# A third PSUM tile for the expert projections of the gate stage, last-norm weights multiplied before the statistics, an early ACT table load

## The chip, the core and the metric

The kernel runs on one core of a Trainium2 chip. The core has a matrix engine (PE, TensorE), three element-wise engines (DVE or VectorE, ACT or ScalarE, POOL or GpSimd) and an engine that issues transfers (SP or SyncE); ACT and POOL issue transfers too. Each engine runs its own instructions in order and waits on semaphores for the others. The metric is the time of one execution on the device, in microseconds (us).

## The reference

One decoder layer on 512 tokens of width 1024 in float32. Cut to what the change touches:

```python
x = x + mix @ w_out                      # mix: short convolution and gated recurrence of norm(x) @ w_in
h2 = rmsnorm(x, norm_ffn)
# peer_ffn(h2): product-key choice of experts, one neuron each
q = (h2 @ wq).reshape(t, 8, 2, 128)
scores = einsum('thpd,hpnd->thpn', q, keys)
s_top, i_top = top_k(scores, 16)         # two halves of 128 keys each
cand = s_top[:, :, 0, :, None] + s_top[:, :, 1, None, :]
c_score, c_idx = top_k(cand, 16)
expert = i1 * 128 + i2                   # one of 16384
gates = softmax(c_score)
a = gelu(einsum('td,thkd->thk', h2, u_tab[expert]))
y = einsum('thk,thkd->td', gates * a, v_tab[expert])
x = x + y
return rmsnorm(x, norm_f)                # x * rsqrt(mean(x*x) + eps) * norm_f
```

## The kernel before

**Numbers.** Matrix products of float32 data are made of three matmuls (`mm3`, L114 to L117): every operand is split into a high part (`hi`) and a rest (`lo`), and hi·hi, hi·lo and lo·hi are added up in PSUM. `split` (L97) does this for a weight tile of 128x1024: ACT copies it into `whi` (L99) and DVE subtracts to give `wlo` (L101).

**Stages.** The first part (up to about 263 us) makes the mixer. A second (to about 369 us) makes the queries and scores, with the top 16 on DVE. Experts are then handled in two ways. For token block 0 the chosen rows of `u_tab` and `v_tab` are gathered one by one: POOL issues an indirect transfer (L675) into a ring of 8 raw slots, and DVE multiplies and adds (L681 for u, L689 for v). For the 384 tokens of blocks 1 to 3 the whole tables are used: `uchunk(c)` (L440) makes Gelu(u·h2) of 128 experts for 384 tokens, 24 matmuls of 128x384 and one ACT Gelu (`gl`, L447), and for early chunks a transfer `Ad<-gl` (L449) spills it. The dense gates for these tokens are built by `gate_m`, 24 times: DVE makes one-hot tables A, B1 and, multiplied by the gate's rest and high part, B2 (L646) and B1 (L647), then PE multiplies them into four PSUM tiles of 8 matmuls each (L656, L657), and ACT evicts each tile into `stg` (L659); every second call sends `stg` to DRAM (L662). Scores and gates live in the pool `psS`, opened before the query loop and closed before the main stage; the chunks U1 to U86 are woven between them. I call 264 to 797 us the gate stage. From about 797 us the main stage multiplies gates and Gelu outputs with `v_tab`, up to 1488.8 us, and `finish` adds the residual and makes the last norm.

**PSUM in the gate stage.** Eight banks: two tiles "a" in `psA`, which the chunks use in turn, and six tiles "m" in `psS` for scores and gates. So the matmuls of chunk n wait for the Gelu of chunk n-2. ACT is in order: that Gelu comes after whatever was put ahead of it, gate evictions and `whi` copies of later chunks among them.

**The order.** The program is written out as loops in the file; a scheduler of the framework then sets the order in which each engine gets its instructions.

**Start and end.** At the start ACT waits for the first piece of the input, loads its function table, scales the input to `hThi` (L155) and copies the first weight. In `finish` (before: L793 to L807) each token block needs, for each half of 512 columns: residual add on DVE (L799), sum of squares on ACT (L800); then the reciprocal root in small steps (`rstd_of`), and a scalar_tensor_tensor (STT) on DVE for each half (L806) that multiplies by the root and by the norm's weights `nfb`.

Of the kernel before, what the change touches and what calls it, by code (L numbers as in the profile page):

```python
# [10 lines left out]
F32 = mybir.dt.float32  # L11
# [4 lines left out]
AF = mybir.ActivationFunctionType  # L16
OP = mybir.AluOpType
AX = mybir.AxisListType
PSUM = bass.MemoryType.PSUM
DRAM = bass.MemoryType.DRAM  # L20

P = 128
T = 512
D = 1024
# [8 lines left out]
TD = T - P  # L33
# [21 lines left out]
def body(ctx, tc, a):  # L55
    nc = tc.nc
    V, S, G, PE = nc.vector, nc.scalar, nc.gpsimd, nc.tensor
# [7 lines left out]
    sm = sb("sm", 2)  # L65
    dr = sb("dr", space=DRAM)
    psA = sb("psA", 2, space=PSUM)
# [9 lines left out]
    ones = const("ones", [P, 2])  # L77
# [16 lines left out]
        V.scalar_tensor_tensor(o, q, 1.5, r, op0=OP.add, op1=OP.mult)  # L94
        return o

    def split(src):  # L97
        hi = ws.tile([P, D], F32R, tag="hi", name="whi")
        S.activation(hi, src, AF.Copy)  # L99
        lo = ws.tile([P, D], F32R, tag="lo", name="wlo")  # L100
        V.tensor_sub(lo, src, hi.bitcast(F32))  # L101
        return hi, lo

    def wunit(src):
# [4 lines left out]
    ring = [None]  # L109
# [6 lines left out]
        PE.matmul(out, l[0], r[1], start=False, stop=False)  # L116
        PE.matmul(out, l[1], r[0], start=False, stop=last)  # L117

    sm.tile([P, 104], F32, name="pad", bufs=1)
    hT = (hp.tile([P, ND, T], F32R, tag="hi", name="hThi"), hp.tile([P, ND, T], F32R, tag="lo", name="hTlo"))  # L120
    x1d = dr.tile([NB, P, D], F32, name="x1d")
    h2d = dr.tile([P, D], F32, name="h2d")
# [23 lines left out]
    wraw = []  # L146
    for i in range(4):
        nc.sync.dma_start(out=xT[i], in_=a["xt"][:, 2 * i:2 * i + 2, :])
        wraw.append(ring[0]())
        nc.sync.dma_start(out=wraw[i], in_=a["w_in"][16 + i])  # L150
    G.memset(ones, 1.0)

    def make_h(dc):
        t = xT[dc // 2][:, dc % 2, :]
# [16 lines left out]
    wf = []  # L171
    for i in range(4):
        make_h(2 * i)
        make_h(2 * i + 1)
        wf.append(split(wraw[i]))
    for t, nm in ((scanm, "scanm"), (maskc, "maskc"), (gmask, "gmask")):
        S.dma_start(out=t, in_=a[nm])
    pf = [ps() for h in range(HG)]
# [46 lines left out]
    for h in range(HG):  # L225
        o = proj(12 + h)
# [17 lines left out]
    for h in range(HG):  # L244
        o = proj(24 + h)
# [143 lines left out]
    c = conv_c(0)  # L389
    for tb in range(NB):  # L390
        hgrn_pre(tb)
    for tb in range(NB):
# [8 lines left out]
        if tb < NB - 1:  # L401
            c = conv_c(tb + 1)
# [3 lines left out]
    nfb = fp.tile([P, D], F32, tag="v", name="nfb")  # L406
# [32 lines left out]

    def uchunk(c):  # L440
        w = wunit(a["u_l"][c])
        o = psA.tile([P, T], F32, tag="a", name="pa")[:, :TD]
        for dc in range(ND):
            sl = slice(dc * P, (dc + 1) * P)
            mm3(o, (w[0][:, sl], w[1][:, sl]), (h2T[0][:, dc, P:], h2T[1][:, dc, P:]), dc == 0, dc == ND - 1)
        gl = mp.tile([P, TD], F32, tag="gl", name="gl", bufs=LAG + 1)
        S.activation(gl, o, AF.Gelu)  # L447
        if c < SPILL:
            S.dma_start(out=Ad[c], in_=gl)  # L449
        return gl  # L450

    h2T = (hp.tile([P, ND, T], F32R, tag="hi", name="h2Thi"), hp.tile([P, ND, T], F32R, tag="lo", name="h2Tlo"))
    h2s = [fp.tile([P, D], F32, tag=t, name="h2s") for t in ("gs", "Q", "G", "E1")]
# [43 lines left out]
    S.dma_start(out=h2n, in_=h2d)  # L497
    G.memset(y0, 0.0)
    sel = ExitStack()
    psS = sel.enter_context(tc.tile_pool(name="psS", bufs=6, space=PSUM))  # L500
    raw_ring(sel.enter_context(tc.tile_pool(name="rs", bufs=1)), 8)
    sp = sel.enter_context(tc.tile_pool(name="sp", bufs=1))
    s2 = sel.enter_context(tc.tile_pool(name="s2", bufs=2))
# [218 lines left out]
    gls = {}  # L722
    for k in range(LAG):
        gls[SPILL + k] = uchunk(SPILL + k)
    sel.close()


# [65 lines left out]
    def finish(tb, ys):  # L793
        xx = xs[tb]
        ms = sm.tile([P, 2], F32, tag="fms", name="fms")
        jk = ring[0]()
        for hf in range(2):
            cs = slice(hf * T, (hf + 1) * T)
            V.tensor_add(xx[:, cs], xx[:, cs], ys[hf])  # L799
            S.activation(jk[:, cs], xx[:, cs], AF.Square, accum_out=ms[:, hf:hf + 1])  # L800
        m = sm.tile([P, 1], F32, tag="m1", name="m1")
        V.tensor_add(m, ms[:, 0:1], ms[:, 1:2])
        r = rstd_of(m, 1.0 / D, 1, "f")
        for hf in range(2):
            cs = slice(hf * T, (hf + 1) * T)
            V.scalar_tensor_tensor(xx[:, cs], xx[:, cs], r[:, 0:1], nfb[:, cs], op0=OP.mult, op1=OP.mult)  # L806
            nc.sync.dma_start(out=a["out"][tb * P:(tb + 1) * P, cs], in_=xx[:, cs])  # L807

    xs = []
    for tb in range(NB):  # L810
# [58 lines left out]
```

## Time and profile before

| | us |
|---|---|
| median of three runs | 1501.52 (1498.21 to 1503.9) |
| the profiled execution, its own time | 1500.03 |
| span of its trace (first to last instruction) | 1498.1 |
| PE busy | 1462.3 (98%) |
| DVE busy | 1201.3 (80%) |
| ACT busy | 637.0 (43%) |
| POOL busy | 365.8 (24%) |
| PE idle on a chunk's Gelu, whole gate stage | 12.4 in 8 waits |

The profiled execution lies 1.5 us under the median of the three runs. Busy shares are an average over stages; "PE busy" counts a matmul that runs at half clock as busy for its whole length, so the granted clock has to be read beside it. A row of a timeline gives the start, the length, the engine, the line, the operation with output and inputs, and in brackets the idle time before it and what ended it.

### The profile page before, as it was taken

To read this page: it belongs to the slowest core of one execution; us is meant where nothing else is said; L and a number is where in the kernel's file an instruction comes from. 1 tells how busy PE (TensorE), PEld (TensorE's weight loads), DVE (VectorE), ACT (ScalarE), POOL (GpSimd) and SP (SyncE) were. 2 spreads that over 40 slices of the span, in tenths; PEclk is the share of its full clock that TensorE was granted. 3 is DMA by queue.
4 is the path that set the end of the run, shared out by engine and by line. 5 is a ranking of instruction groups with operands and counts; after the bars stand their busy time and mean duration, and the time that the engine had idled before them with its cause. 6 is when DMAs were issued, how large, how long until landed. Compare 5 with 4: busy or idle time off the path is not lost.

```text
span 1498.1 us, 21741 instructions
## 1 busy us (share of the span) xinstructions
PE 1462.3 (98%) x7929; PEld 1297.3 (87%) x7929; DVE 1201.3 (80%) x2312; ACT 637.0 (43%) x900; POOL 365.8 (24%) x284
## 2 busy tenths in 40 slices
PE   7999999999998999999999999999999999999997
PEld 6887777888998998889999999999998888888886
DVE  5847876799989988788829878778787788888887
ACT  5833324333443365666744333333333333333333
POOL 0000000000034142320014445444343224333340
PEclk9999999999999999999999999999999999999999
DMA  6231233622469789689779999998989999999993
GB/s 230 85 106 43 70 127 112 246 86 90 161 209 386 244 279 315 231 293 321 261 287 419 324 337 323 338 341 313 345 298 338 368 369 368 355 356 352 352 342 118
DMA packets 137770, 394.64 MB, mean 263 GB/s; under 512 B 13120, under 2 KB 59584, under 8 KB 135488
## 3 DMA queue, kind: packets, MB, share of 16 engines
q1 hardware_dynamic: 47520, 170.94, 31.5%
q0 software_dynamic: 39168, 159.40, 29.4%
q10 hardware_dynamic: 50976, 62.93, 11.9%
q8 instruction: 62, 1.02, 0.3%
q14 instruction: 44, 0.36, 0.1%
HBM read 346.82 MB, written 46.40 MB: 262 GB/s over the span
## 4 chain that ended last, share of the span: by engine, by line
PE 76%; DVE 6%; ACT 5%; issue 5%; DMA 5%; POOL 2%; ACTq 1%; POOLq 0%; DVEq 0%
PE y L116 10%; PE y L115 10%; PE y L117 10%; PE pa L115 8%; PE pa L116 7%; PE pa L117 7%; PE pm L115 7%; PE pm L116 6%; PE pm L117 6%; ACT stg L659 4%; DMA wraw<-in_v_dram,e_i 2%; POOL wraw L675 2%; DVE wlo L101 2%; DMA wraw<-in_u_dram,e_i 1%; PE pm L538 1%
## 5 line engine op out<-in xcount | busy, mean ns | idle before, releaser
L99 ACT ACTIVATE whi<-wraw 128x1024 fp32r<-128x1024 f32 x308 | 325.8, 1058 | 518.4 <-PE pa L116 205.4
L101 DVE TENSOR_TENSOR wlo<-wraw,whi 128x1024 fp32r<-128x1024 f32 x308 | 376.2, 1222 | 144.8 <-ACT whi L99 141.1
L115 PE MATMUL pa<-h2Thi,whi 128*128 128x384 f32 x1024 | 348.0, 340 | 12.7 <-ACT gl L447 12.4
L117 PE MATMUL pa<-h2Thi,wlo 128*128 128x384 f32 x1024 | 346.6, 338 | 0.0
L116 PE MATMUL pa<-h2Tlo,whi 128*128 128x384 f32 x1024 | 346.2, 338 | 0.0
L675 POOL DMA_INDIRECT wraw<-in_u_dram,e_i x128 | 183.3, 1432 | 490.2 <-DVE ci L523 178.6
L116 PE MATMUL y<-wlo,wh 128*128 128x512 f32 x768 | 299.5, 390 | 0.0
L115 PE MATMUL y<-whi,wh 128*128 128x512 f32 x768 | 298.9, 389 | 0.2 <-ACT wh L747 0.2
L117 PE MATMUL y<-whi,wl 128*128 128x512 f32 x768 | 296.8, 390 | 0.0
L675 POOL DMA_INDIRECT wraw<-in_v_dram,e_i x128 | 169.4, 1323 | 263.2 <-DVE wlo L101 122.0
L115 PEld LDWEIGHTS pa<-h2Thi,whi 128*128 128x128 f32 x1024 | 194.3, 190 | 17.8 <-ACT gl L447 15.9
L116 PEld LDWEIGHTS pa<-h2Tlo,whi 128*128 128x128 f32 x1024 | 194.4, 190 | 1.6
L117 PEld LDWEIGHTS pa<-h2Thi,wlo 128*128 128x128 f32 x1024 | 194.1, 190 | 0.0
L681 DVE SCALAR_TENSOR_TENSOR wraw<-wraw,h2n 128x1024 f32<-128x1024 f32 x128 | 155.9, 1219 | 34.7 <-DMA wraw<-in_u_dram,e_i 34.6
L689 DVE SCALAR_TENSOR_TENSOR y<-wraw,w,y 128x1024 f32<-128x1024 f32 x128 | 163.9, 1280 | 17.1 <-DMA wraw<-in_v_dram,e_i 16.9
L117 PEld LDWEIGHTS y<-whi,wl 128*128 128x128 f32 x768 | 144.1, 188 | 30.2
L115 PEld LDWEIGHTS y<-whi,wh 128*128 128x128 f32 x768 | 144.2, 188 | 29.7 <-ACT wh L747 0.6
L116 PEld LDWEIGHTS y<-wlo,wh 128*128 128x128 f32 x768 | 144.1, 188 | 29.0
L747 ACT ACTIVATE wh<-w 128x384 fp32r<-128x384 f32 x128 | 65.8, 522 | 208.2 <-PE y L116 97.6
L659 ACT ACTIVATE stg<-pm 128x512 f32<-128x512 f32 x96 | 92.3, 1156 | 17.7 <-PE pm L657 17.7
L749 DVE TENSOR_TENSOR wl<-w,wh 128x384 fp32r<-128x384 f32 x128 | 70.2, 554 | 22.8 <-ACT wh L747 22.3
L115 PE MATMUL pm<-hThi,whi 128*128 128x512 f32 x192 | 77.7, 406 | 8.4 <-ACT whi L99 8.4
(240 smaller groups left out, 1694.7 us busy)
## 6 DMA issues: line engine op xcount, KB each, us to landing
wraw<-in_u_l_dram SPq DMA_DIRECT2D x128, 512.0 KB, 5.6
wraw<-in_v_l_dram SPq DMA_DIRECT2D x128, 512.0 KB, 6.4
Gd<-stg ACTq DMA_DIRECT2D x12, 2048.0 KB, 7.6
Gt<-Gd POOLq DMA_DIRECT2D x16, 1536.0 KB, 9.7
Ad<-gl ACTq DMA_DIRECT2D x84, 192.0 KB, 5.0
glr<-Ad ACTq DMA_DIRECT2D x84, 192.0 KB, 5.2
wraw<-in_w_in_dram SPq DMA_DIRECT2D x24, 512.0 KB, 3.7
wraw<-in_wq_dram SPq DMA_DIRECT2D x16, 512.0 KB, 7.4
```

The costliest lines, as they stand in the source:

```text
L99: S.activation(hi, src, AF.Copy)
L101: V.tensor_sub(lo, src, hi.bitcast(F32))
L115: PE.matmul(out, l[0], r[0], start=first, stop=False)
L116: PE.matmul(out, l[0], r[1], start=False, stop=False)
L117: PE.matmul(out, l[1], r[0], start=False, stop=last)
L538: PE.matmul(o[:, tb * NK:(tb + 1) * NK], q[:, tb * P:(tb + 1) * P], keys[:, i, :], start=True, stop=True)
L659: S.activation(st[:, t0:t0 + 4, :], o3, AF.Copy, scale=1.0 / GSC)
L675: G.indirect_dma_start(out=t, out_offset=None, in_=a[tab], in_offset=bass.IndirectOffsetOnAxis(ap=e_i32[:, j:j + 1], axis=0))
L681: V.scalar_tensor_tensor(r, r, 1.0, h2n, op0=OP.mult, op1=OP.mult, accum_out=act0[:, j:j + 1])
L689: V.scalar_tensor_tensor(y0, r, w0[:, j:j + 1], y0, op0=OP.mult, op1=OP.add)
L747: S.activation(wh, w, AF.Copy)
L749: V.tensor_sub(wl, w, wh.bitcast(F32))
```

## The change

1. `psS` gets five banks for scores and gates. The sixth becomes a tile "u", and while the gate stage lasts every third chunk (c % 3 == 2) uses it; the other chunks go on using the two tiles of `psA`. Chunk n then waits for the Gelu of the chunk three before it.
2. In `finish` both halves of x are multiplied by `nfb` into a second buffer `xm` (from the same raw ring) as soon as the residual is added. After the root, half 0 is scaled on DVE by a tensor_scalar and half 1 on ACT by a Copy with a scale.
3. A tiny ACT Copy of `ones` stands ahead of everything that waits for data, so that ACT's table is loaded there. The first weight is split in four pieces of 256 columns. A pad tile shrinks from 104 to 96 columns.

```diff
-    def split(src):
+    def split(src, n=1):
         hi = ws.tile([P, D], F32R, tag="hi", name="whi")
-        S.activation(hi, src, AF.Copy)
         lo = ws.tile([P, D], F32R, tag="lo", name="wlo")
-        V.tensor_sub(lo, src, hi.bitcast(F32))
+        for i in range(n):
+            cs = slice(i * D // n, (i + 1) * D // n)
+            S.activation(hi[:, cs], src[:, cs], AF.Copy)
+            V.tensor_sub(lo[:, cs], src[:, cs], hi[:, cs].bitcast(F32))
         return hi, lo
...
-    sm.tile([P, 104], F32, name="pad", bufs=1)
+    sm.tile([P, 96], F32, name="pad", bufs=1)
...
     G.memset(ones, 1.0)
+    S.activation(sm.tile([P, 2], F32, name="warm", bufs=1), ones, AF.Copy)
...
-        wf.append(split(wraw[i]))
+        wf.append(split(wraw[i], 1 if i else 4))
...
     def uchunk(c):
         w = wunit(a["u_l"][c])
-        o = psA.tile([P, T], F32, tag="a", name="pa")[:, :TD]
+        o = upsum(c)[:, :TD]
...
+    in_sel = [False]
+
+    def upsum(c):
+        if in_sel[0] and c % 3 == 2:
+            return psS.tile([P, T], F32, tag="u", name="pa", bufs=1)
+        return psA.tile([P, T], F32, tag="a", name="pa")
...
-    psS = sel.enter_context(tc.tile_pool(name="psS", bufs=6, space=PSUM))
+    psS = sel.enter_context(tc.tile_pool(name="psS", bufs=5, space=PSUM))
+    in_sel[0] = True
...
+    in_sel[0] = False
     sel.close()
...
     def finish(tb, ys):
         xx = xs[tb]
         ms = sm.tile([P, 2], F32, tag="fms", name="fms")
-        jk = ring[0]()
+        jk, xm = ring[0](), ring[0]()
         for hf in range(2):
             cs = slice(hf * T, (hf + 1) * T)
             V.tensor_add(xx[:, cs], xx[:, cs], ys[hf])
             S.activation(jk[:, cs], xx[:, cs], AF.Square, accum_out=ms[:, hf:hf + 1])
+            V.tensor_mul(xm[:, cs], xx[:, cs], nfb[:, cs])
...
-            V.scalar_tensor_tensor(xx[:, cs], xx[:, cs], r[:, 0:1], nfb[:, cs], op0=OP.mult, op1=OP.mult)
-            nc.sync.dma_start(out=a["out"][tb * P:(tb + 1) * P, cs], in_=xx[:, cs])
+            if hf:
+                S.activation(xm[:, cs], xm[:, cs], AF.Copy, scale=r[:, 0:1])
+            else:
+                V.tensor_scalar(xm[:, cs], xm[:, cs], r[:, 0:1], None, op0=OP.mult)
+            nc.sync.dma_start(out=a["out"][tb * P:(tb + 1) * P, cs], in_=xm[:, cs])
```

The lines after the change have other numbers: about 3 more in the first part (L155 becomes L158, L447 becomes L450), 11 more in the gate stage (L646 becomes L657, L659 becomes L670).

Where the order changes, first ACT at the start of the program, before and then after. `warm` is the new tiny copy, `E` the buffer for squares.

```order
L145 DMA prm<-in_prm_dram 128x33
L145 DMA ident<-in_ident_dram 128x128
L177 DMA scanm<-in_scanm_dram 128x512
L155 ACT_TABLE_LOAD
L155 ACTIVATE hThi<-F,prm 128x512 x2
L177 DMA maskc<-in_maskc_dram 128x128
L177 DMA gmask<-in_gmask_dram 128x128
L99 ACTIVATE whi<-wraw 128x1024
```

```order
L147 DMA prm<-in_prm_dram 128x33
L147 DMA ident<-in_ident_dram 128x128
L154 ACT_TABLE_LOAD
L154 ACTIVATE warm<-ones 128x2
L180 DMA scanm<-in_scanm_dram 128x512
L158 ACTIVATE hThi<-F,prm 128x512 x2
L180 DMA maskc<-in_maskc_dram 128x128
L180 DMA gmask<-in_gmask_dram 128x128
L102 ACTIVATE whi<-wraw 128x256 x4
```

The table load now stands ahead of everything that waits for `F`, and one transfer, `scanm`, has gone behind it.

Second, ACT at the first pair of gate calls, before and then after: `stg<-pm` is the eviction of a gate tile, `gl<-pa` a chunk's Gelu.

```order
L99 ACTIVATE whi<-wraw 128x1024
L447 ACTIVATE gl<-pa 128x384
L449 DMA Ad<-gl 128x384
L659 ACTIVATE stg<-pm 128x4x128 x8
L99 ACTIVATE whi<-wraw 128x1024
L662 DMA Gd<-stg 128x16x256
L447 ACTIVATE gl<-pa 128x384
```

```order
L102 ACTIVATE whi<-wraw 128x1024
L450 ACTIVATE gl<-pa 128x384
L452 DMA Ad<-gl 128x384
L670 ACTIVATE stg<-pm 128x4x128 x5
L102 ACTIVATE whi<-wraw 128x1024
L670 ACTIVATE stg<-pm 128x4x128
L450 ACTIVATE gl<-pa 128x384
L670 ACTIVATE stg<-pm 128x4x128 x2
L452 DMA Ad<-gl 128x384
L673 DMA Gd<-stg 128x16x256
```

The eight evictions in a row have become five, with a weight copy and a Gelu among the last three.

Third, DVE at the seventh and eighth gate call, before and then after: `A` and `B` are the one-hot tables, `y` the v rows of block 0, `oh` work on the next block's choice.

```order
L605 TENSOR_TENSOR oh<-oh 128x32x8
L644 TENSOR_TENSOR A<-iota,gt 128x2048
L645 TENSOR_TENSOR B_5087<-iota,gt 128x2048
L689 SCALAR_TENSOR_TENSOR y_2163<-wraw,w_2161,y_2163 128x1024
L644 TENSOR_TENSOR A<-iota,gt 128x2048
L645 TENSOR_TENSOR B_5206<-iota,gt 128x2048
L646 TENSOR_TENSOR B_5088<-B_5087,gt 128x2048
L101 TENSOR_TENSOR wlo<-wraw,whi 128x1024
```

```order
L616 TENSOR_TENSOR oh<-oh 128x32x8
L655 TENSOR_TENSOR A<-iota,gt 128x2048
L656 TENSOR_TENSOR B_5095<-iota,gt 128x2048
L700 SCALAR_TENSOR_TENSOR y_2171<-wraw,w_2169,y_2171 128x1024
L657 TENSOR_TENSOR B_5096<-B_5095,gt 128x2048
L655 TENSOR_TENSOR A<-iota,gt 128x2048
L656 TENSOR_TENSOR B_5214<-iota,gt 128x2048
L658 TENSOR_TENSOR B_5095<-B_5095,gt 128x2048
```

The seventh call's first product (L646 before, L657 after) has moved ahead of the eighth call's two tables.

## Rows read from the trace of the kernel before

**Rows 1.** First page: busy time by engine.

```profile
PE 1462.3 (98%) x7929; PEld 1297.3 (87%) x7929; DVE 1201.3 (80%) x2312; ACT 637.0 (43%) x900; POOL 365.8 (24%) x284
```

**Rows 2.** What PE waited for, 430 to 765 us: total, times, longest.

```profile
PE pa L115 <- ACT gl L447: 12.4, 8, 4.2
PE pm L656 <- DVE B L646: 1.8, 1, 1.8
```

**Rows 3.** The first of these, 702 to 765 us alone.

```profile
PE pa L115 <- ACT gl L447: 2.0, 2, 1.6
```

**Rows 4.** Stretches: busy us by engine (instructions), granted clock, DMA share, GB/s.

```profile
454.50:461.30 6.80, 5.03 (x16) 5.03 (x17) 6.80 (x18) 2.20 (x3) 3.22 (x3) 0.50 0.95 350
461.30:500.00 38.70, 38.70 (x225) 38.67 (x224) 36.29 (x65) 14.31 (x20) 10.96 (x7) 1.00 0.99 374
635.40:642.30 6.90, 6.10 (x21) 5.79 (x22) 6.90 (x7) 2.18 (x4) 1.27 (x1) 0.51 1.06 403
```

**Rows 5.** Timeline of PE at the two longest waits on a Gelu.

```profile
451.76 0.34 PE L117 MATMUL pa<-h2Thi,wlo 128*128 128x384 f32 x1
456.27 0.69 PE L115 MATMUL pa<-h2Thi,whi 128*128 128x384 f32 x1 [4.17 <-ACT gl L447]
...
636.20 0.69 PE L115 MATMUL pa<-h2Thi,whi 128*128 128x384 f32 x1 [3.19 <-ACT gl L447]
```

**Rows 6.** Timeline of ACT and its queue at the same two places.

```profile
453.16 0.31 ACT L565 ACTIVATE g<-g 128x128 f32<-128x128 f32 x1 [6.41 <-DVE g L564]
...
628.53 6.08 ACTq L449 DMA_DIRECT2D Ad<-gl  x1
634.71 1.06 ACT L99 ACTIVATE whi<-wraw 128x1024 fp32r<-128x1024 f32 x1 [5.26 <-issue]
```

**Rows 7.** Timelines of PE and DVE at two gate calls.

```profile
593.51 0.40 PE L656 MATMUL pm<-B,A 128*128 128x128 f16 x4 [1.79 <-DVE B L646]
...
592.24 1.22 DVE L646 TENSOR_TENSOR B<-B,gt 128x2048 f16<-128x2048 f16 x1
...
701.65 0.40 PE L656 MATMUL pm<-B,A 128*128 128x128 f16 x4
...
699.96 2.35 DVE L646 TENSOR_TENSOR B<-B,gt 128x2048 f16<-128x2048 f16 x2
```

**Rows 8.** What DVE waited for, 453 to 702 us (first four).

```profile
DVE wraw L681 <- DMA wraw<-in_u_dram,e_i: 19.7, 7, 4.9
DVE y L689 <- DMA wraw<-in_v_dram,e_i: 5.7, 3, 4.5
DVE A L644 <- ACT gt L629: 4.3, 2, 3.1
DVE wlo L101 <- ACT whi L99: 3.0, 6, 0.9
```

**Rows 9.** Timelines of POOL and DVE at one gather.

```profile
543.53 9.03 POOL L675 DMA_INDIRECT wraw<-in_u_dram,e_i  x1 [10.57 <-DVE y L689]
...
556.12 1.23 DVE L681 SCALAR_TENSOR_TENSOR wraw<-wraw,h2n 128x1024 f32<-128x1024 f32 x1 [4.37 <-DMA wraw<-in_u_dram,e_i]
```

**Rows 10.** Timeline of ACT: the first pair of gate calls.

```profile
529.75 7.75 ACT L659 ACTIVATE stg<-pm 128x512 f32<-128x512 f32 x8 [2.60 <-PE pm L657]
```

**Rows 11.** Timelines of ACT and PE at the start.

```profile
4.73 1.28 ACT L155 ACT_TABLE_LOAD   x1 [4.73 <-DMA F<-in_xt_dram]
6.03 1.33 ACT L155 ACTIVATE hThi<-F,prm 128x512 fp32r<-128x512 f32 x2
7.27 1.04 ACT L99 ACTIVATE whi<-wraw 128x1024 fp32r<-128x1024 f32 x1
...
8.36 0.79 PE L115 MATMUL pm<-hThi,whi 128*128 128x512 f32 x1 [8.36 <-ACT whi L99]
```

**Rows 12.** Timeline of DVE at the end.

```profile
1490.74 1.41 DVE L806 SCALAR_TENSOR_TENSOR wraw<-wraw,vo,nfb 128x512 f32<-128x512 f32 x2
...
1493.52 1.41 DVE L806 SCALAR_TENSOR_TENSOR wraw<-wraw,vo,nfb 128x512 f32<-128x512 f32 x2
```

## The prediction

> **What bounds the kernel now.** I read the first page first: it says which engine fills the span. PE is busy 98% of it and the next engine, DVE, 80% [rows 1]. So a change gains only what it takes from PE's idle time, from stretches in which PE runs at half clock, or from the start and end where PE has nothing to do. The list of PE's waits comes next. Between 430 and 765 us, in the gate stage, PE stood 12.4 us in 8 waits for a chunk's Gelu (`gl`), and 1.8 us once for a gate table of DVE [rows 2]. The windows of the same stage show a second loss: right after the two long waits the granted clock is 0.50 and 0.51, the 1.2 GHz level, where the stretch after the first has 1.00 [rows 4]. Before each of these falls PE had stood idle, 4.17 and 3.19 us by its timeline [rows 5].
>
> The two timelines of ACT say why PE stood. At the first place ACT itself waited 6.41 us for DVE to deliver `g`, the gate's softmax input, and the Gelu that PE needed came after it, so that PE went on at 456.27 [rows 5, 6]. At the second place the issue of one spill transfer took 6.08 us, and ACT's next instruction began at 634.71 [rows 6]. Neither has to do with PE. PE was stopped because a chunk may begin only when the Gelu of the chunk two before it is done. In both cases it would have had other chunks to do.
>
> **Part 1, the third tile: the ceiling.** A chunk is 24 matmuls; in the stretch from 461.3 us at full clock PE did 225 in 38.70 us, 0.172 us each [rows 4], so a chunk is some 4.1 us of PE work. With three tiles a Gelu may be one chunk later before PE stops. The stalls are 4.17 and 3.19 us and smaller ones, so almost all of the 12.4 us would go; of the first I leave 0.3 us, since ACT must also copy the weights of the chunk that PE would run in the gap. What the low clock costs: between 454.5 and 461.3 PE was busy 5.03 us, between 635.4 and 642.3 it was busy 6.10 us [rows 4], and at half clock half of that is lost, 2.5 and 3.05 us. Ceiling: 12.4 - 0.3 + 2.5 + 3.05 = 17.7 us.
>
> **Why I take less.** PE can be earlier only if what else it needs is earlier too. In this stage it also needs the gate tables of DVE, and DVE is in order and has its own waits. At 593.51 PE already waits 1.79 us for a table that DVE ends 592.24 + 1.22 = 593.46; at 701.65 it starts on one whose two products run from 699.96 to 702.31, of which the first ends about 701.1, so PE has about half a microsecond in hand there [rows 7]. The change puts this first product about 2.3 us earlier on DVE, but the gate matmuls about 2.6 us earlier on PE too, so the margin stays. What is gained before 593 or before 702 is then kept only as far as DVE also comes earlier. DVE's waits say how far that can be. Between 453 and 702 us 25.4 us (19.7 + 5.7) are waits for gathered rows, 3.0 us for `whi` and 4.3 us for `gt`, both from ACT [rows 8]. The waits for `whi` end earlier with PE, since a `whi` buffer comes free when PE is done with it: 3.0 us. The waits for `gt` hang on PE (transposes) and ACT: I take 3 of 4.3. The gathers I take as staying as they are: their transfers are issued by POOL as DVE frees the slots, and one of them needed 9.03 us to be issued while DVE worked on [rows 9]. So up to 702 us the gain is 3 + 3 = 6 us. Behind 702 the stalls on Gelus are 2.0 us [rows 3], with no near table in the way; they are added. **Gate stage: -8 us**, bounds -3 (only the waits for `whi`) and -17.7 (ceiling). Between ends so far apart I take the value nearer to the low one, because the row at 593.51 shows the cap already reached before the change.
>
> On the 9.03 us, the Trainium skill (SBUF — State Buffer, the box on "DVE blocks DMA" under "two separate sides") says that descriptors of a transfer issued by GpSimd cannot be written while VectorE runs an operation in a two-port mode, and that the transfer then appears blocked. By that rule the gathers would follow DVE wherever it goes, and its 25.4 us would not shrink. The trace agrees only in part: the issue spans DVE's work and ends where DVE stops and waits 4.37 us, yet a later section of the page doubts that the operations DVE runs there count.
>
> **Part 1, the price: a bank fewer for the gates.** Two gate calls make eight tiles in a row; ACT evicted the eight in 7.75 us, 0.97 us each [rows 10]. With five banks the sixth tile waits for the first eviction. In the new order matmuls of a chunk stand ahead of the sixth tile, about six of them, 6 x 0.172 = 1.0 us, as much as one eviction takes. That is the work that hides it; with that cover I price it at nothing. Without it each pair would lose up to two evictions, 1.9 us. ACT's order moves the same way: five evictions together, then a weight copy and a Gelu among the others. The scores of the stage before share these five banks; I price that at nothing too, since the same evictions and the same cover hold there, and a loss belongs to the slower rival below.
>
> **Part 3, the start.** ACT got its table at 4.73, after waiting for the first input, and that load took 1.28 us [rows 11]. Now it lies in the wait for data, so the first copies are 1.28 us earlier. The first weight copy took 1.04 us as one [rows 11]; in quarters PE can begin after the first, some 0.6 us sooner, an estimate. PE would then begin at about 6.5 in place of 8.36. But PE runs out of weights again: each further weight needs about 3.4 us of ACT (two input copies 1.33, the weight 1.04 [rows 11], and a square of the weight's shape, the same again by estimate), and its transfer besides, which comes no earlier. Bounds 0 and -1.9; I take -0.6. The Trainium skill (ScalarE: Activation LUTs, "What ACT_TABLE_LOAD costs") gives some 2.66 us for a switch, with a drain; by that the upper bound would be -3.3. The trace disagrees: the load is 1.28 us, and the next copy starts 1.30 us after it began [rows 11].
>
> **Part 2, the end.** The last block's two STTs took 1.41 us [rows 12]. A tensor_scalar on DVE and a Copy on ACT, side by side, take about half, so -0.7. Against it stand two extra multiplications per block, at an STT's half of 0.7 us each; those of the last block run while ACT squares and takes the root. The block before loses its pair of STTs too (1.41 us at 1490.74) and gains one tensor_scalar, and DVE runs it in order ahead of the last block's root. I take -0.3; bounds -0.7 and +1.4 (both multiplications not hidden).
>
> **Sum.** -8 - 0.6 - 0.3 = -8.9 us. Against the profiled execution: 1500.0 - 8.9 = 1491.1, span 1498.1 to 1489.2. The median of the runs lies 1.5 us above the profiled one, so the predicted median is 1501.5 - 8.9 = 1492.6, rounded to **1492.5 us**. A measurement can tell about 0.5%, 7.5 us, from no change; the forecast lies just beyond.
>
> **The rivals.**
> - *The full ceiling.* DVE comes earlier as well, because its gathers are issued earlier along with it and the waits for `gt` go. For it: DVE waits there, it isn't full (80%) [rows 1]. Against it: PE's wait at 593.51. Gain 13 to 17.7 plus 0.9: around 1485 us.
> - *VectorE keeps its pace.* What PE gains on Gelus it gives back as longer waits for tables, and a longer wait for a table may drop the clock just as the waits on Gelus did. Then the gate stage gains 0 to 5, of it 2.0 behind 702 for certain. For it: the wait at 593.51, the margin at 701.65 and the 25.4 us of gather waits; the rule of the skill above would make it so. Time 1496 to 1501, with 1498.5 in the middle.
> - *Slower: five gate banks are too few.* The cover of chunk matmuls fails, because those matmuls themselves wait, or ACT's evictions come later behind the weight copy that now stands between them. Price: two evictions of 0.97 us per pair, 12 pairs, 23.3 us; with -8.9 from the rest +14.4, about 1516 us. It decides when a pair loses over 8.9 / 12 = 0.74 us; slower by over 0.5% from (8.9 + 7.5) / 12 = 1.4 us per pair.
> - *The tile doesn't do what it says.* If chunks wait for operands rather than for the Gelu, the third tile stays empty. Against it: where PE stood before a chunk, the wait list names the Gelu, 12.4 us of it, and never `whi` or `wlo` [rows 2]. Its time is that of the second rival's upper end, and its chance lies there.
>
> **How the numbers follow.** My forecast (gate stage gains 5 to 13): 0.50. Full ceiling: 0.12. VectorE keeps its pace: 0.30. Slower by five banks, at any size: 0.08. Faster by over 0.5% needs a gain over 7.5 us: all of the ceiling, 0.12, and three quarters of the forecast's chance, 0.38, which gives 0.50. Within 0.5%: the rest of the forecast, 0.12, and the second rival, 0.30, which gives 0.42. Slower 0.08. The range runs from 1484 (near the ceiling's 1501.5 - 18.6 = 1482.9, the last of it left out) to 1502 (the second rival with nothing gained and something lost at the end); the slower rival and the tip of the ceiling stay outside, about 1 in 10. The forecast's own range, for gate gains of 5 to 13, is 1487.6 to 1495.6.
>
> **What would show it.** In the list of PE's waits the Gelu falls from 12.4 us to 1 or so, and waits for gate tables of DVE grow from 2 to 5 to 10 us; if they don't grow, the ceiling holds. The half-clock stretches near 454 and 635 go, or come back behind a wait for a table. DVE's waits for gathers in the stage stay near 25 us. The sixth tile of a pair doesn't show a wait for an eviction; if it does in most pairs, the slower rival holds. At the start PE begins near 6.5; at the end the last output follows the last matmul by a little less. The prediction is wrong if the gate stage, from the first chunk to the main stage, is shorter by under 5 or over 13 us.

## The result and the profile after

| | before | after |
|---|---|---|
| median | 1503.54 us (1498.21 to 1505.03, 6 runs) | 1493.79 us (1492.01 to 1496.41, 6 runs) |
| profiled execution | 1500.03 us, span 1498.1 | 1494.14 us, span 1491.9 |

The ratio is 0.994, with a 95% interval of 0.9923 to 0.9956: 9.75 us by the medians, where 8.9 were forecast. The two profiled executions stand only 5.9 us apart, because that of before is on the fast side of its runs. The trace answers for these two executions. I cut them at four places that both have: the first matmul of chunk U1, the 145th matmul into a `y` tile (a point in the main stage with the same 2927 matmuls behind it in both), the end of the last matmul, and the end of the span.

| stretch | before, us | after, us | difference |
|---|---|---|---|
| start to U1 | 363.57 | 362.19 | -1.38 |
| gate stage, U1 to the 145th `y` matmul | 499.65 | 492.41 | -7.24 |
| from there to the last matmul's end | 625.58 | 628.63 | +3.05 |
| last matmul's end to the span's end | 9.30 | 8.67 | -0.63 |
| sum | 1498.10 | 1491.90 | -6.20 |

From here on "gate stage" is the second of these stretches; a list of waits names its own window.

Busy time, first page of the kernel after (it answers to [rows 1]): 

```profile
PE 1460.3 (98%) x7929; PEld 1292.9 (87%) x7929; DVE 1200.9 (80%) x2319; ACT 639.6 (43%) x908; POOL 368.7 (25%) x284
```

The shares don't move, so nothing is to be read from them. What PE waited for does move; the same list, 430 to 765 us, for the kernel after (answers to [rows 2]; total, times, longest):

```profile
PE pm L667 <- DVE B L657: 5.5, 3, 2.2
PE pa L117 <- ACT gl L450: 1.7, 1, 1.7
PE pm L668 <- DVE B L658: 1.5, 2, 1.3
PE pa L119 <- DVE wlo L103: 0.5, 1, 0.5
```

Waits on a Gelu are down from 12.4 us to 1.7. Waits on the gate tables are up from some 2 to 5.5 + 1.5 = 7.0 us. No wait on the eviction of a gate tile is in the list. The windows at half clock (they answer to [rows 4]):

```profile
467.00:470.40 3.40, 3.40 (x13) 3.40 (x12) 3.40 (x11) 1.98 (x3) 0.54 (x1) 0.50 1.04 420
586.40:589.80 3.40, 3.08 (x13) 3.09 (x14) 3.40 (x4) 0.82 (x2) 0.00 (x0) 0.50 1.08 408
```

Two stretches of 3.40 us are left of two of 6.8. PE was busy 3.40 + 3.08 us in them and lost half, 3.2 us, where it had lost 5.6. Both still come behind a wait of PE, as its timeline shows, the first on a Gelu, the second on a table. Not every wait is followed by one: behind those of 1.77, 1.27 and 1.48 us between 634 and 655 us the granted clock stayed at 1.00.

```profile
465.28 0.44 PE L117 MATMUL pa<-h2Thi,whi 128*128 128x384 f32 x1 [1.74 <-ACT gl L450]
...
586.72 0.50 PE L667 MATMUL pm<-B,A 128*128 128x128 f16 x3 [2.24 <-DVE B L657]
```

These terms give the stage: Gelus -10.7, tables +4.9, `wlo` +0.5, clock -2.3, together -7.6, against -7.24 measured.

At the first of the two old stalls ACT stands as long as before, but PE no longer does. Timeline of ACT after (answers to [rows 6]):

```profile
451.37 0.31 ACT L576 ACTIVATE g<-g 128x128 f32<-128x128 f32 x1 [6.00 <-DVE g L575]
...
463.80 1.06 ACT L102 ACTIVATE whi<-wraw 128x1024 fp32r<-128x1024 f32 x1 [1.94 <-DMA wraw<-in_u_l_dram]
```

ACT's wait of 6.00 us for `g` was covered. A short one came 14 us later, when PE had run ahead of the weights' transfers and ACT waited for them; the DMA engines were full there (share 1.04 in the window at 467 above).

The late tables stand behind gathered rows. In VectorE's timeline the table of the wait at 586.72 ends 586.66, and since its 4.12 us for a row VectorE has not paused:

```profile
579.49 1.23 DVE L692 SCALAR_TENSOR_TENSOR wraw<-wraw,h2n 128x1024 f32<-128x1024 f32 x1 [4.12 <-DMA wraw<-in_u_dram,e_i]
...
585.44 1.22 DVE L657 TENSOR_TENSOR B<-B,gt 128x2048 f16<-128x2048 f16 x1
```

The other three of over 1 us come the same way, without a pause of VectorE in between: those at 634.78 and 641.60 behind a wait of 4.21 us for a row that ended at 621.21, that at 653.67 behind one of 3.97 us that ended at 646.65.

In the main stage PE has two waits that before did not have (list, 797 to 1485 us). The first, at 1134.81, stands behind a row of block 0 that VectorE waited 4.01 us for, the second, at 1140.18, behind that and a load of gates (`Gt`, 0.80 us). They are 3.0 us, against +3.05 for the stretch:

```profile
PE y L119 <- DVE wl L761: 1.5, 1, 1.5
PE y L117 <- ACT wh L759: 1.5, 1, 1.5
```

Start and end, timelines of ACT, PE and DVE after (answer to [rows 11, 12]):

```profile
1.67 1.28 ACT L154 ACT_TABLE_LOAD   x1 [1.67 <-PEq L877]
4.93 0.72 ACT L158 ACTIVATE hThi<-F,prm 128x512 fp32r<-128x512 f32 x1 [1.77 <-DMA prm<-in_prm_dram]
6.17 1.32 ACT L102 ACTIVATE whi<-wraw 128x256 fp32r<-128x256 f32 x4
...
6.63 0.79 PE L117 MATMUL pm<-hThi,whi 128*128 128x512 f32 x1 [6.63 <-ACT whi L102]
...
1486.78 0.49 DVE L822 TENSOR_SCALAR wraw<-wraw,vo 128x512 f32<-128x512 f32 x1
...
1485.92 1.58 ACT L820 ACTIVATE wraw<-wraw,vo 128x512 f32<-128x512 f32 x2 [0.18 <-issue]
```

The table load lies in the wait for data, and PE begins 1.73 us earlier. The last block's scaling is 0.49 us on DVE beside 0.72 on ACT, in place of 1.41. It ends 4.27 us after the last matmul, in place of 6.13, so 1.86 us sooner; the span's end gains only 0.63. The DMA share says where the rest stays: after, the last six outputs follow each other without a pause and fill the DMA engines, where before there were gaps between them. First the kernel after, then before:

```profile
1486.00:1490.00 4.00, 0.00 (x0) 0.00 (x0) 1.13 (x6) 1.36 (x2) 0.00 (x0) 0.69 1.02 390
...
1492.00:1494.00 2.00, 0.00 (x0) 0.00 (x0) 1.50 (x8) 0.20 (x1) 0.00 (x0) 0.54 0.68 262
1494.00:1495.00 1.00, 0.00 (x0) 0.00 (x0) 0.94 (x2) 0.00 (x0) 0.00 (x0) 0.50 0.00 0
```

### The profile page after: what moved, and what is told of

The parts are those of the page before. It is cut to its first block, busy times and chain, and to the rows that moved or that the text cites. A ratio compares the mean times of both kernels' runs of the same rounds, so it can differ in the third digit from the quotient of the medians.

```text
span 1491.9 us, 21767 instructions
## 1 busy us (share of the span) xinstructions
PE 1460.3 (98%) x7929; PEld 1292.9 (87%) x7929; DVE 1200.9 (80%) x2319; ACT 639.6 (43%) x908; POOL 368.7 (25%) x284
## 4 chain that ended last, share of the span: by engine, by line
PE 46%; issue 7%; DMA 5%; POOL 2%; DVE 2%; ACT 0%; POOLq 0%; ACTq 0%; DVEq 0%
PE y L117 10%; PE y L119 10%; PE y L118 10%; PE pa L119 5%; PE pa L118 5%; PE pa L117 5%; DMA wraw<-in_v_dram,e_i 3%; POOL wraw L686 2%; DMA wraw<-in_u_dram,e_i 1%; PE pm L667 1%; PE pm L668 1%; DMA Gt<-Gd 1%; DVE wlo L103 0%; DMA wraw<-in_v_l_dram 0%; DVE B L656 0%
## 5 line engine op out<-in xcount | busy, mean ns | idle before, releaser
L102 ACT ACTIVATE whi<-wraw 128x1024 fp32r<-128x1024 f32 (+1 forms) x311 | 325.9, 1049 | 506.6 <-PE pa L118 189.6
L103 DVE TENSOR_TENSOR wlo<-wraw,whi 128x1024 fp32r<-128x1024 f32 (+1 forms) x311 | 376.0, 1210 | 142.1 <-ACT whi L102 133.5
L700 DVE SCALAR_TENSOR_TENSOR y<-wraw,w,y 128x1024 f32<-128x1024 f32 x128 | 163.7, 1279 | 14.1 <-DMA wraw<-in_v_dram,e_i 13.7
L670 ACT ACTIVATE stg<-pm 128x512 f32<-128x512 f32 x96 | 94.3, 1159 | 19.2 <-PE pm L668 19.1
```

Of the source, the lines that this page charges most:

```text
L102: S.activation(hi[:, cs], src[:, cs], AF.Copy)
L103: V.tensor_sub(lo[:, cs], src[:, cs], hi[:, cs].bitcast(F32))
L670: S.activation(st[:, t0:t0 + 4, :], o3, AF.Copy, scale=1.0 / GSC)
L700: V.scalar_tensor_tensor(y0, r, w0[:, j:j + 1], y0, op0=OP.mult, op1=OP.add)
```

## The experiments

Twelve kernels, each against runs of the kernel before on the same chip. The last columns are read from each one's trace as in the table above; "half clock" is the time at 0.50 between 264 and 797 us.

| kernel | ratio (95%) | median, us | gate stage, us | half clock, us |
|---|---|---|---|---|
| before | 1 | 1502.4 to 1503.5 | 499.65 | 13.6 |
| after | 0.994 (0.9923 to 0.9956) | 1493.79 | 492.41 | 6.8 |
| p1_tile | 0.9942 (0.9927 to 0.9957) | 1492.54 | 490.88 | 3.4 |
| p23_ends | 0.998 (0.9967 to 0.9993) | 1500.29 | 499.94 | 10.2 |
| five_banks | 0.9949 (0.9937 to 0.9962) | 1495.75 | 495.54 | 10.2 |
| four_banks | 0.9963 (0.9946 to 0.998) | 1497.32 | 497.14 | 13.6 |
| two_u | 0.9926 (0.9898 to 0.9954) | 1491.13 | 489.78 | 3.4 |
| light_b1 | 0.99 (0.9885 to 0.9916) | 1489.17 | 492.31 | 13.6 |
| no_gather | 0.9841 (0.9813 to 0.9868) | 1477.75 | 478.72 | 0 |
| no_gather_b | 0.9895 (0.9878 to 0.9912) | 1487.30 | 485.20 | 0 |
| early36 | 1.0063 (1.0042 to 1.0084) | 1510.63 | 487.42 | 3.4 |
| lag2 | 0.9952 (0.9933 to 0.9972) | 1493.90 | 492.06 | 6.8 |
| lag2_two | 0.9946 (0.9927 to 0.9965) | 1493.04 | 488.51 | 3.4 |
| lag1_two | 0.994 (0.9919 to 0.9962) | 1492.95 | 490.76 | 3.4 |

How far can one trace be trusted? lag2 runs the instructions of the kernel after on PE, ACT, DVE and POOL in the same order, one for one; its gate stage is 492.06 us against 492.41. two_u, lag1_two and lag2_two share another order: 489.78, 490.76 and 488.51. So between single traces of this stage a difference of some 2 us shows nothing.

### The parts alone

The third tile alone (p1_tile) is the kernel after with the old start and `finish`:

```diff
-            V.tensor_mul(xm[:, cs], xx[:, cs], nfb[:, cs])
...
-    S.activation(sm.tile([P, 2], F32, name="warm", bufs=1), ones, AF.Copy)
...
-        wf.append(split(wraw[i], 1 if i else 4))
+        wf.append(split(wraw[i]))
```

> Only the third PSUM tile and the five gate banks; start and end as before. Theory (the gain comes from the gate stage, where PE no longer stands for a Gelu two chunks back, cut short by VectorE's tables): first matmul at 8.36 us as before, PE's waits on a chunk's Gelu at most 3 us in place of 12.4, its waits on gate tables 5 to 10 us, chunk U85 begins 6 to 8 us earlier than before, and the time is 6 to 9 us under before. Rival (the gain is mainly in the start and the end): under 3 us gained.

Measured: 0.9942, ten us under before by the medians, the gate stage 8.8 us shorter. PE's waits (430 to 765 us) are 0.4 us on Gelus, 6.3 on tables and 2.4 on a weight. That is as much as the whole change gives.

Start and end alone (p23_ends) are the kernel after without the tile:

```diff
-    psS = sel.enter_context(tc.tile_pool(name="psS", bufs=5, space=PSUM))
-    in_sel[0] = True
+    psS = sel.enter_context(tc.tile_pool(name="psS", bufs=6, space=PSUM))
```

> Only the early table load, the first weight in four pieces and the new finish; PSUM as before. Theory: first matmul near 6.6 us, the first chunk after the scores begins about 1.4 us earlier than before, the end after the last matmul is 8.7 us in place of 9.3, PE's waits on a chunk's Gelu stay at 10 to 14 us, and the time is about 2 us under before (1 to 3). Rival (the start is lost again before the gate stage because the weights come no earlier): at most 1 us.

Measured: 0.998, some 3 us by the ratio, with an interval from 1 to 5. First matmul at 6.63, end 8.83 us after the last matmul. But U1 began at 363.58, as before: of the 1.73 us nothing was left there. The clock goes some way to explain it. In the trace of p23_ends the windows around 137 and 164 us have

```profile
137.00:140.40 3.40, 3.40 (x10) 2.63 (x10) 3.40 (x7) 0.30 (x1) 0.00 (x0) 0.50 0.04 14
164.40:167.80 3.40, 3.40 (x9) 2.61 (x9) 3.40 (x6) 0.10 (x1) 0.00 (x0) 0.52 0.00 0
```

and in that of before the first of them is at 1.00:

```profile
137.00:140.40 3.40, 3.40 (x31) 3.02 (x30) 3.40 (x10) 1.26 (x2) 0.00 (x0) 1.00 0.36 142
```

From 125 us up to the fall at 137 PE's timeline of p23_ends has no wait. The traces sort by this: with the new start U1 begins at 359.7 to 359.85 where there are 3.4 us of half clock between the start's and U1 (light_b1, no_gather, lag2_two), at 362.2 to 362.4 with 10.2 us (after, lag2), at 363.6 to 363.9 with 13.6 us (p23_ends, two_u, lag1_two, early36). With the old start and 10.2 us it begins at 363.57 to 364.20 (before, five_banks, four_banks). At equal clock, 10.2 us, the start earns 1.2 to 2.0 us. The clock does not explain all of it: with the old start and only 6.8 us U1 begins at 363.29 and 363.36 (p1_tile, no_gather_b).

### The bank taken away, without the tile

```diff
-    psS = sel.enter_context(tc.tile_pool(name="psS", bufs=6, space=PSUM))
+    psS = sel.enter_context(tc.tile_pool(name="psS", bufs=5, space=PSUM))
```

> The kernel before with five PSUM banks for scores and gates and the sixth left unused. Theory (chunk matmuls ahead of the sixth tile hide the wait for an eviction): within 3 us of before, PE's waits on an eviction of a gate tile under 2 us in all. Rival (a bank fewer costs up to two evictions of 0.97 us per pair of gate calls): 10 to 23 us slower, with a wait on an eviction in most of the 12 pairs; then the third tile earns that much more than the sum shows.

Neither theory. It is 0.9949, some 7 us faster, by taking a bank away and using it for nothing. PE's waits in the gate stage of five_banks:

```profile
PE pm L656 <- DVE B L646: 5.4, 4, 1.8
PE pa L115 <- issue: 3.6, 1, 3.6
PE pa L115 <- ACT gl L447: 0.7, 2, 0.4
PE pm L657 <- DVE B L647: 0.5, 1, 0.5
```

The small waits on Gelus are all but gone with two chunk tiles as well (0.7 us); the first long one is left (3.6, at 452 us; the list names no engine for it, but ACT waits 5.88 us for the input of `g` there as before), and the tables have taken up 5.9. The timeline of ACT at the first pair of gate calls shows what moved (answers to [rows 10]):

```profile
530.25 4.86 ACT L659 ACTIVATE stg<-pm 128x512 f32<-128x512 f32 x5 [2.69 <-PE pm L657]
534.89 1.08 ACT L99 ACTIVATE whi<-wraw 128x1024 fp32r<-128x1024 f32 x1
535.87 1.10 ACT L659 ACTIVATE stg<-pm 128x512 f32<-128x512 f32 x1
536.75 0.54 ACT L447 ACTIVATE gl<-pa 128x384 f32<-128x384 f32 x1
```

With six banks the scheduler put eight evictions in a row, 7.75 us in which no Gelu could run. With five it puts a weight copy and a Gelu between them. In the trace of before five of PE's eight waits on a Gelu, 4.9 us of the 12.4, come right behind such a row, a weight copy and the Gelu; the longest of them, timelines of ACT and PE before:

```profile
665.30 7.72 ACT L659 ACTIVATE stg<-pm 128x512 f32<-128x512 f32 x8 [3.15 <-PE pm L657]
672.76 1.11 ACT L99 ACTIVATE whi<-wraw 128x1024 fp32r<-128x1024 f32 x1
673.71 0.53 ACT L447 ACTIVATE gl<-pa 128x384 f32<-128x384 f32 x1
...
674.29 0.45 PE L115 MATMUL pa<-h2Thi,whi 128*128 128x384 f32 x1 [1.62 <-ACT gl L447]
```

The two long ones do not: they are the wait for `g` and the issue of a spill. Taking away one more bank (`bufs=4`, four_banks):

> The kernel before with four PSUM banks for scores and gates, two left unused; two tiles for the chunks as before. Theory (long runs of evictions on ACT hold up the chunks' Gelus; fewer banks break the runs up): as with five banks or better, 5 to 10 us under before, PE's waits on a Gelu or its queue at most 5 us, runs of evictions on ACT of four or fewer. Rival (five banks were a lucky order of the scheduler; each bank taken away costs evictions): 3 us or more slower than with five banks.

Measured 0.9963: not more than with five, its interval overlapping that of five_banks. The gate stage is 2.5 us shorter than before in place of 4.1; waits on tables are 8.2 us, on Gelus 4.1. ACT has eleven rows of eight evictions before, five with five banks (the same rows as in the kernel after, one for one) and two with four. So breaking up still more of them brings nothing more. That the order is what helps is read from ACT's timeline; a bank less also reorders VectorE, and no run keeps that as it was.

### More tiles for the chunks

```diff
-        if in_sel[0] and c % 3 == 2:
-            return psS.tile([P, T], F32, tag="u", name="pa", bufs=1)
+        if in_sel[0] and c % 4 >= 2:
+            return psS.tile([P, T], F32, tag="u", name="pa", bufs=2)
...
-    psS = sel.enter_context(tc.tile_pool(name="psS", bufs=5, space=PSUM))
+    psS = sel.enter_context(tc.tile_pool(name="psS", bufs=4, space=PSUM))
```

> The changed kernel with four banks for scores and gates and two extra chunk tiles, so that chunk n waits for the Gelu of chunk n-4. Theory (with the Gelu waits gone the tables of VectorE are what is left, and they don't come earlier): within 2 us of the changed kernel, waits on Gelus near 0, waits on gate tables 6 to 10 us. Rival (the slack of a fourth tile lets PE run over VectorE's lateness as well): 3 us or more under the changed kernel. If four banks are too few, it is slower and the waits are on evictions.

Measured 1491.13 us, 2.7 under the kernel after by the medians, with intervals that overlap: it can't be told from it. No wait on a Gelu is left in the gate stage; waits on tables are 6.4 us and on weight copies (`whi`, 465 to 469 us) 2.7. A fourth tile does not get PE past VectorE, nor past the weights.

### What makes the tables late

One table operation of four left out of each gate call (the gates are then not scaled):

```diff
-        V.tensor_mul(B1, B1, view(2))
```

> The changed kernel without one of the four table operations of each gate call, the product of B1 with the gate's high part; the gates are then not scaled. VectorE has 24 operations of 1.14 us, some 27 us, less to do in the gate stage, and PE the same. Theory (VectorE's tables cap what the third tile gives): PE's waits on gate tables fall from 7.0 us to under 2 us, the half-clock stretch behind such a wait goes, and the time is 5 to 9 us under the changed kernel. Rival (PE is bound by its own work and by Gelus and weights, the tables' lateness only follows PE): at most 3 us under the changed kernel, with waits on Gelus in the tables' place.

Measured 0.99, 4.6 us under the kernel after by the medians and 6.0 by the ratios, whose intervals don't meet. The time is near the theory's, but not where the theory had it: the gate stage of its trace is 492.31 us, the same as after. VectorE did less and waited more. Its waits between 453 and 702 us:

```profile
DVE wraw L691 <- DMA wraw<-in_u_dram,e_i: 26.6, 8, 8.1
DVE y L699 <- DMA wraw<-in_v_dram,e_i: 12.2, 2, 6.7
```

Its shorter total in this trace comes from elsewhere, 2.3 us ahead at U1 by the clock and 1.9 us in the main stage; what shortens its other runs one trace doesn't show. The waits are 38.8 us on gathered rows, where the kernel after has 14.9 + 4.6 = 19.5. One of them, 8.1 us, made a table 6.91 us late for PE. In this trace, then, the gathered rows in VectorE's queue set the tables' time and not its amount of work; the order of evictions and gathers has changed too, so the kernel does not settle it. The next kernel takes the gathers of this stage away and keeps VectorE's 48 operations on them, which the scheduler then puts earlier (no_gather; the rows are missing from the result):

```diff
-        r = rows("u", j)
-        V.scalar_tensor_tensor(r, r, 1.0, h2n, op0=OP.mult, op1=OP.mult, accum_out=act0[:, j:j + 1])
+        r = h2n if in_sel[0] else rows("u", j)
+        V.scalar_tensor_tensor(ring[0]() if in_sel[0] else r, r, 1.0, h2n, op0=OP.mult, op1=OP.mult, accum_out=act0[:, j:j + 1])
...
-        r = rows("v", j)
+        r = h2n if in_sel[0] else rows("v", j)
```

> The changed kernel without the 48 gathers of the gate stage: VectorE runs the same 48 operations, but on a tile that is there already, so that nothing waits for a gathered row; the result then lacks these rows, and the scheduler puts the operations earlier. Theory (VectorE, in order, stands behind gathered rows, 19.5 us in the changed kernel, and so its tables come late): PE's waits on gate tables fall from 7.0 us to 3 us or less, and the time is 3 to 8 us under the changed kernel. Rival (VectorE's amount of work makes the tables late): within 2 us of the changed kernel, tables still 5 us or more.

Measured 1477.75 us, 16 under the kernel after, twice the theory's most. PE's waits, whole gate stage:

```profile
PE pm L637 <- ACT stg L670: 0.3, 1, 0.3
PE pm L668 <- DVE B L658: 0.2, 1, 0.2
```

No stretch at half clock is left in it either. But the edit takes away more than VectorE's waits: 48 transfers of 512 KB, POOL's issues, and some of the ring slots that the chunks' weights use too. The windows from 430 to 500 us and ACT's waits for these weights (430 to 765 us) show it, the kernel after first and then no_gather:

```profile
430.00:500.00 70.00, 67.75 (x381) 67.08 (x380) 65.23 (x139) 27.41 (x37) 29.96 (x23) 0.98 0.97 352
ACT whi L102 <- DMA wraw<-in_u_l_dram: 11.3, 5, 4.5
...
430.00:500.00 70.00, 70.00 (x406) 70.00 (x405) 69.26 (x153) 30.55 (x41) 0.00 (x0) 1.00 0.58 189
ACT whi L102 <- DMA wraw<-in_u_l_dram: 1.5, 1, 1.5
```

That the gathers cost this time is shown. That they do so mainly through VectorE's queue is argued: from VectorE's timeline above, and from PE's list of the kernel after, where tables have 7.0 us and weights 0.5. The same edit on the kernel before (no_gather_b):

> The kernel before (two chunk tiles, six banks, old start and end) without the 48 gathers of the gate stage, VectorE running the same 48 operations on a tile that is there already; the result lacks these rows. It stands beside the changed kernel without gathers (1477.75 us). Theory (the third tile is worth its ceiling, 12 to 18 us in the gate stage, once the gathers no longer make VectorE's tables late; with them it keeps about half): the gate stage is 10 to 18 us longer than in the changed kernel without gathers, PE's waits on Gelus at least 8 us, about 1490 us in all. Rival (the gathers alone were the loss and the third tile adds nothing without them): within 5 us of the changed kernel without gathers, no Gelu waits of note.

Between the two. It is 9.5 us over no_gather by the medians, with 5.5 us of waits on Gelus in 6 pieces, the longest 1.54; the gate stage is 6.5 us longer, where I had said 10 to 18. The two long waits on a Gelu went with the gathers, and what stood behind them went too: ACT no longer waits for `g`, and the longest issue of a spill is 1.48 us in place of 6.08. Before `g` VectorE had waited 4.5 us for rows (430 to 453 us); why a spill's issue takes so long beside gathers is open. The gathers cost the stage 13.7 us with the third tile (492.41 to 478.72) and 14.5 us with two (499.65 to 485.20). The tile, with the bank that it takes, is worth 6.5 us without them and 7.24 with them (the latter with the half clock).

### Ways to put the gathers elsewhere

```diff
-EARLY = 48
+EARLY = 36
-PACE = (2.65, 1.1)
+PACE = (2.95, 1.1)
```

> The changed kernel with 36 in place of 48 gathered rows in the gate stage and 12 more in the first part of the main stage. Theory (gathers cap the gate stage): the gate stage shrinks by 2 to 6 us through fewer waits on gate tables; the main stage, where PE has no wait in sight and VectorE is busy some 82%, stays, so 2 to 5 us under the changed kernel. Rival (the main stage pays): waits of PE on wh or wl of 2 us or more appear there, and the sum is within 2 us or slower.

The first half is as the theory has it, the gate stage 5.0 us shorter. The rival has the sum: 1.0063. PE's waits in the main stage:

```profile
PE y L117 <- ACT wh L759: 12.9, 7, 3.5
```

The order of the second part changed as well: the last six of the seven are 1.56 to 1.61 us each and come every 34.5 us, where the `w` products of four chunks are now made in one go.

Gathers used two later than issued (the kernel after, or two_u, with a list of held rows):

```diff
+    def gu(j):
+        held.append((use_u, j, rows("u", j)))
...
+            while len(held) > (2 if in_sel[0] else 0):
+                f, j, r = held.pop(0)
+                f(j, r)
```

> The changed kernel with the same 48 gathers in the gate stage, each used two gathers later in the program than it is issued. Theory (VectorE, in order, stands for rows that land late because POOL's issue takes 5 to 9 us at times): VectorE's waits on gathered rows between 453 and 702 us fall from 19.5 to under 10 us, PE's waits on gate tables from 7.0 to under 4, and the time is 3 to 8 us under the changed kernel. Rival (slots held longer delay the chunk loads or POOL's issues, so the rows land later too): within 2 us or slower, gather waits still 15 us or more.

> Both, four chunk tiles with four gate banks and gathers used two later. Theory: the two add up, 4 to 10 us under the changed kernel, about 1484 to 1490 us, which would be the fastest here. Rival: as the four chunk tiles alone, 1491 us.

> Four chunk tiles with four gate banks and gathers used one later. Theory: between the four tiles alone (1491 us) and the lag of two, 1486 to 1490 us. Rival: no different from the four tiles alone.

The rivals hold. lag2 is 1493.90 us, with 16.3 + 3.4 = 19.7 us of waits on gathered rows, as after. The scheduler orders VectorE by its own times, not by the program's order, and put the uses back where they were: the order of PE, ACT, DVE and POOL is that of the kernel after in lag2, and that of two_u in lag2_two and lag1_two (1493.04 and 1492.95). So these kernels don't test whether a longer lead would help; they are the same work measured again, and two_u's lead does not come back in them. No kernel here with the reference's whole computation is shown to beat the kernel after.

## Why the prediction was right, and where a step of it was not

The forecast was 1492.5 us in a range of 1484 to 1502, and the time is 1493.79.

**The ceiling, and what was given back.** That PE would give part of the ceiling back on tables was right. Waits on tables went from 2 to 7.0 us, within the 5 to 10 named; the gate stage gained 7.24 us where I had said 8. The clock's loss did not go whole, since two shorter waits brought it back.

**Why the tables are late: half right.** I capped the gain by DVE's waits that could shrink, 3.0 us on `whi` and 3 of 4.3 on `gt`, and let the gathers stay at 25.4. The runs say otherwise. In the kernel after the gather waits fell to 19.5, while those on `gt` are 3.6 and those on `whi` rose to 5.9. That the gathers make the tables late is borne out by VectorE's timeline and no_gather together; how much of it goes through VectorE's queue is argued. That they set how much the third tile may gain is not: it is worth about the same without them. The second argument failed, and the 8 us came near by a sum whose pieces were off.

**The price of the bank: the sign.** I priced the missing bank at nothing and saw in it only a rival that makes the kernel slower. It is itself worth 4.1 us of the gate stage (five_banks), and the third tile another 4.7 on top of it (495.54 to 490.88 in p1_tile), each by single traces; the ratios of p1_tile and five_banks, 0.9942 and 0.9949, can't be told apart. My order rows had shown the eight evictions broken into five and three with a Gelu among them; I read that as a cover for the bank, not as the removal of what made the smaller Gelu waits. The slower rival is out: PE waits on no eviction in the kernel after.

**Start and end.** -0.6 was mis-sized: the first matmul moved by 1.73 of the 1.9 named as the bound, and at equal clock 1.2 to 2.0 us reach U1; the feed by ACT takes little back. How much a single execution shows is in part set by where the clock falls. The end gave -0.63 (-0.47 in p23_ends) against -0.3, near its bound of -0.7. The scaling itself came 1.86 us sooner; that the outputs' transfers would then set the end was not in the term. Nor is the gain clear of the other traces: with the new `finish` this stretch runs from 8.3 to 10.5 us, with the old one from 9.3 to 10.1. On the table load the trace after agrees with the one before: 1.28 us, and `warm` begins at 2.97, 1.30 after it began. That a switch costs 2.66 us with a drain (the Trainium skill, ScalarE: Activation LUTs, "What ACT_TABLE_LOAD costs") the trace does not show: all 21 loads of the kernel after take 1.28 us, and in all but one, which waits for `g`, ACT's next instruction begins 1.29 to 1.34 us after the load began.

**A term that was missing.** I took the main stage as fixed. Over these traces the stretch from the 145th `y` matmul to the last runs from 625.6 to 629.2 us, leaving out early36, mostly by one or two waits of 1 to 2 us; the profiled execution of before had the shortest of all. That would explain why the profiled executions differ by less than the medians; one trace of before can't show it. Without this stretch the pieces come to -9.25 us, near the medians' -9.75; with it to -6.2. So the nearness of 8.9 to 9.75 is in part luck: the start and the end gave more than was said, the gate stage less.

## What to carry to other kernels

Before giving a waiting engine more buffers, ask what holds up the engine that frees them: here runs of eight evictions on ACT did for 4.9 of the 12.4 us, and breaking them up with fewer buffers for the evictions earned about as much in the gate stage as the third tile on top of it, as far as single traces tell. A wait that one engine loses comes back on the next thing that is late, so the gain is the wait less what the next one lets through. Where a schedule is made by a program, a change of a count is also a change of order: run the count alone, without the thing it was changed for.

## What was not expected of the hardware

**A gather's issue beside an unbroken run of VectorE.** The timeline of POOL, and of DVE's last operation in the run, in the kernel after:

```profile
539.56 9.02 POOL L686 DMA_INDIRECT wraw<-in_u_dram,e_i  x1 [10.39 <-DVE y L700]
548.88 0.94 POOL L686 DMA_INDIRECT wraw<-in_v_dram,e_i  x1 [0.31 <-issue]
...
547.49 0.28 DVE L616 TENSOR_TENSOR oh<-oh 128x256 f16<-128x256 f16 x1
552.15 1.23 DVE L692 SCALAR_TENSOR_TENSOR wraw<-wraw,h2n 128x1024 f32<-128x1024 f32 x1 [4.38 <-DMA wraw<-in_u_dram,e_i]
```

From 539.2 to 547.77 DVE ran nine operations with no pause, and the issue ended 0.8 us after the last; the next one, with DVE idle, took 0.94. The long issues of before (9.03 and 8.29 us) came back at 9.02 and 8.29 in the kernel after and at 9.03 and 8.29 in lag2, each beside the same operations of DVE's, if not quite in the same order. But another issue of the kernel after did not wait, though DVE ran the same kind of operation (L657) beside it all the time:

```profile
516.22 0.93 POOL L686 DMA_INDIRECT wraw<-in_v_dram,e_i  x1 [0.30 <-issue]
...
516.23 2.38 DVE L657 TENSOR_TENSOR B<-B,gt 128x2048 f16<-128x2048 f16 x2
```

The Trainium skill (SBUF — State Buffer, the "DVE blocks DMA" box) has such a lock for VectorE's two-port modes. The long issues agree with it in that they end behind DVE's run, though the run is made of TENSOR_TENSOR operations, for which the page's section "Who interferes with whom" doubts it; the issue at 516.22 speaks against it. No run here took that cause away alone, so it is argued and not shown.

**Half clock without a wait.** In the first 264 us stretches at 0.50 come near 137, 163, 188 or 254 us, from one to three of them. Only the one near 254 follows a long wait of PE (3.1 us for `h2s`). What brings the others is open. The program does not decide it: two_u, lag1_two and lag2_two run the same instructions in the same order and have 13.6, 13.6 and 3.4 us of half clock before U1, which begins at 363.84, 363.92 and 359.70. Such 4 us in a single execution are no effect of a change.
